# Conditioning vectors of a two-layer diffusion step: dot products spread out, part of them on the matrix engine, deeper weight splitting

## The chip, the cores and the metric

The program runs on one core of a Trainium2 chip. The engines of that core work in parallel, each on its own queue in order: TensorE (PE, with its weight loads shown apart as PEld), VectorE (DVE), ScalarE (ACT), GpSimd (POOL) and SyncE (SP), which here issues almost all transfers. The metric is device time in microseconds (us); lower is better. Three runs of the kernel before took 2530.45, 2533.19 and 2536.13 us, so the median is 2533.19 us.

## The reference

One inference step of a backbone with two layers and a width of D = 2048, over 128 context tokens and 128 latent tokens (256 columns in all). Cut to what matters here:

```
def modulation(cond, w_mod_l, b_mod_l):              # six vectors of 2048 numbers for each
    m = silu(cond) @ w_mod_l + b_mod_l               # layer and each of two conditions
    return split(m, 6)            # shift1, scale1, gate1, shift2, scale2, gate2

def trunk_layer(x, mod, ...):
    q_r, k_r, v_r, g_r, q_a, k_a, v_a = split(modulate(x, shift1, scale1) @ w_in_l)
    y_r = retention_output(...)                      # 8 heads, two directions
    y_a = windowed attention with a sink             # 8 query heads, 2 key/value heads
    x = x + gate1 * (concat(y_r, y_a) @ w_out_l)
    x = x + gate2 * conv_ffn(modulate(x, shift2, scale2), w_up_l, conv_w_l, conv_b_l, w_down_l)
    return x, k_a, v_a, states

modulate(x, shift, scale) = rms_norm(x) * (1 + scale) + shift
```

All of it is float32. The conditioning matrix `w_mod` alone has 2 x 2048 x 12288 numbers, a third of all weights that are read.

## The kernel before, in words

Activations lie transposed: `xT` holds 16 chunks of 128 features by 256 tokens. Each weight matrix is cut into 128 x 128 tiles, 16 tiles to a **unit** of 1 MB that one DMA brings into a slot of `raw` (RAWB = 6 slots, issued in order on SP, each as soon as a slot is given back), and 8 tiles to a **piece**. There are 768 pieces in the program and two pieces in each unit. A float32 product is made of three faster ones: the weight piece is split into a rounded part `hi` (ACT, line 440) and the rest `lo` (DVE, line 441), the operand `hT` (or `ypair`) likewise into columns 0 to 255 and 256 to 511, and `triple` (lines 585 to 587) multiplies hi by hi, hi by lo and lo by hi. So a piece is 24 matmuls of 256 columns. `split_upto` runs LOOK = 2 pieces ahead of the piece being multiplied, and LOOK + 1 = 3 slots hold the split pieces.

The stages follow one another in an order written out in `events`: in each layer the input projection by heads ("kv", "q", "ret"; 88 pieces), the output projection ("out", 32), and three times an up projection ("up", 64, 64 and 48 pieces) and a down projection ("down", 32, 32 and 24). Between "out" and "up", and between the layers, stands a **norm**: the last output chunk is added to `xT` and squared, `norm1` sums the squares on PE (line 478), takes the root on POOL, and `norm2` spreads the factor over the partitions (line 490). Then `emit_h` makes `hT` chunk by chunk, and the first 16 pieces after a norm (two weight groups side by side, `duo_piece`) take the chunks as they come. Smaller work of the heads is done in steps: `step_side` after each piece runs one step of a queue of tasks (`kv_task`, `q_task`, `ret_task`), whose matmuls into `aux` stand in PE's queue between pieces.

The six conditioning vectors of each layer are made in two ways.

- **On PE** (`emit_mod0`, `emit_mod`, lines 359 and 373): a load of 1 MB of `w_mod` is multiplied by the condition, with four matmuls of 512 columns that stand on four strips of 32 columns of the array. Layer 0's first two vectors take 32 such loads before and during the first 48 pieces, gate1 of each layer takes 16 loads more, one at a time.
- **On DVE** (`emit_dot`, line 382): 128 outputs need two dot products (one for each condition) of 2048 products; a load of 1 MB serves both. There are 128 loads and 256 such instructions, for the other eight vectors. `dots` lists them in the order of use, and `dknots` and `quota` say how many must have been issued by which piece. While `hT` is made after a norm none is issued; what the quota asks for by then comes at once behind the last of these pieces.

Of the kernel before, what the change touches and what calls it, by code (L numbers as in the profile page):

```python
# [26 lines left out]
LOOK = 2  # L27
RAWB = 6
# [93 lines left out]
PESEQ = [(0, 2), (1, 2)]  # L122
DVESEQ = [(0, 4), (0, 3), (0, 5), (1, 1), (1, 0), (1, 4), (1, 3), (1, 5)]
# [3 lines left out]
def body(ctx: ExitStack, tc: tile.TileContext, io):  # L127
# [5 lines left out]
    mods = [(l, v, u) for l, v in PESEQ for u in range(MU)]  # L133
    dots = [(l, v, u, k) for l, v in DVESEQ for u in range(KC) for k in range(2)]
# [6 lines left out]
    def mod_event():  # L141

        if issued[0] < len(mods):
            events.append(("mod", mods[issued[0]]))
# [12 lines left out]
    knots = [(ahead, 0), (gstart["out", 0] - 2, MU), (gstart["kv", 1], MU), (gstart["out", 1] - 2, 2 * MU)]  # L157
    nd = 2 * KC
    dknots = [(ahead // 3, 0), (gstart["up", 0] - 4, 2 * nd), (gstart["down", 0] - 6, 3 * nd),
              (gstart["kv", 1] - 6, 11 * nd // 2), (gstart["up", 1] - 4, 7 * nd), (gstart["down", 1] - 6, 8 * nd)]  # L160
# [8 lines left out]

    def startup(b, i):  # L170
        for h in range(MU // 8):
            events.append(("mod0", (0, 1 - i // 2, b, MU // 8 * (i % 2) + h)))
# [14 lines left out]
    for j, p in enumerate(pieces):  # L187
        g = groups[p["it"]["g"]]
        kind, l = g["kind"], g["l"]
        if "gb" in p["it"] and p["first"]:  # L190
            w = 0 if kind == "kv" else 1
            start = j
            events.append(("norm1", None))
            events.append(("norm2", None))
# [4 lines left out]
        if "gb" in p["it"]:  # L199
            for _ in range(2 if (j - start) % 3 == 2 else 1):  # L200
                if chunks:
                    hs.append(chunks.popleft())
            hs = (l, w, hs)
# [29 lines left out]
    for ev, arg in events:  # L233
        if ev in ("mod", "mod0"):
# [28 lines left out]
    dump = one.tile([P, D], BF16, name="dump")  # L263
# [22 lines left out]
    def pump():  # L286
        while nload[0] < len(loads):
# [10 lines left out]
            else:  # L298
                src = io["w_" + key[0]]
                if key[0] == "mod0":  # L300
                    at = key[1]
                else:
                    l, v, u = key[1]
                    at = ((PESEQ if key[0] == "mod" else DVESEQ).index((l, v)), u)
# [20 lines left out]
    def close_mod(ps, l, v, b=None):  # L325

        mod_fin()
        ev = tp.tile([P, 512], F32, tag="t2", name="mev", bufs=3)
# [20 lines left out]
    def emit_mod0(v, b, h):  # L349

        key = ("mod0", (0, v, b, h))
# [11 lines left out]
        if h == MU // 4 - 1:  # L363
            close_mod(md[0], 0, v, b)
# [22 lines left out]
    def end_dots(l, v):  # L387
        dst = modT[l][:, v, :, :]
        bias = C("bmod", l * 96 + v * KC, KC)
        nc.vector.tensor_tensor(dst, dst, bias.unsqueeze(2).to_broadcast([P, KC, 2]), op=ALU.add)  # L390
        if v in (1, 4):
            nc.vector.tensor_scalar_add(dst, dst, 1.0)
# [95 lines left out]
    def norm2():  # L488
        ps = aux()
        nc.tensor.matmul(ps[:, 0:256], ones, diag[0], start=True, stop=True)  # L490
        nc.scalar.copy(rb, ps[:, 0:256])

    hu = {}

    def emit_hu(l, w, kcs, ahead=True):

        m = modT[l]
        for kc in kcs:
# [5 lines left out]
            for s in range(2):  # L504
                a = slice(P * s, P * s + P)
                nc.vector.scalar_tensor_tensor(u[:, a], xT[:, kc, a], m[:, 3 * w + 1, kc, s:s + 1], rb[:, a],
                                               op0=ALU.mult, op1=ALU.mult)

# [21 lines left out]
    def emit_piece(j):  # L530
# [10 lines left out]
        if p["first"]:  # L541
            cur.clear()
            cur["ps"] = [ps_m.tile([P, 512], F32, tag="m", name="acc") for _ in range(2)]
# [3 lines left out]
        for i, (n, kc) in enumerate(p["tiles"]):  # L547
            c = cur["n"]
            out = cur["ps"][n // 2][:, 256 * (n % 2):256 * (n % 2) + 256]
            c[n] += 1  # L550
            src = Y(kc) if g["kind"] in ("out", "down") else hT[:, kc, :]
            triple(out, j, i, src, c[n] == 1 and n % 2 == 0, c[n] == nk)
            if c[n] == nk and n % 2 == 1:
                fin.append(n)
# [3 lines left out]
        for n in fin:  # L558
            evac(gi, g, n, cur["ps"][n // 2])
# [69 lines left out]

    def evac(gi, g, n, ps):  # L630
# [12 lines left out]
        else:  # L643
            nt = g["ns"][n - 1]
            v = 2 if kind == "out" else 5
            t = tp.tile([P, 512], F32, tag="t2", name="gx", bufs=3)
# [389 lines left out]
```

## Time and profile before

| what | value |
|---|---|
| median of three runs | 2533.19 us |
| the profiled execution, its own time | 2530.89 us |
| its span, first to last instruction | 2529.1 us |
| mean granted TensorE clock | 0.979 |
| PE busy | 2381.1 us, 94% |
| DVE busy | 1985.7 us, 79% |
| ACT busy | 1175.9 us, 46% |
| bytes moved | 619.36 MB, mean 245 GB/s |

The profiled execution spends 1.8 us outside its span. A busy engine is not proof of a bound: matmuls overlap, so PE counts as busy as long as one is in flight. What a stage loses is read by comparing it with a like stage that has no wait. "PEclk" is the share of full clock granted to TensorE; its two levels are 2.4 GHz (1.0) and 1.2 GHz (0.5).

### The profile page before, as it was taken

Reading aid. Unit: us, or ns where it says so; the run is one execution under the profiler, and the core shown is the slowest. Engines: PE = TensorE matmul, PEld = TensorE weight load, DVE = VectorE, ACT = ScalarE, POOL = GpSimd, SP = SyncE. Lnnn points to the kernel's source line nnn. Section 1 sums busy time; section 2 is a strip of 40 time slices with the busy share of each in tenths; the row PEclk is TensorE's granted clock in tenths of the full one; section 3 lists DMA queues with packets and bytes.
Section 4 is the critical chain, followed back from the end, with each engine's and each line's share of the span. In section 5 each row is a group of like instructions: output and inputs, shape, how many; then the busy total and the mean of one; then the engine's idle time right before and its main releaser. Section 6 shows DMA issues by size and latency. Waiting matters only on the chain.

```text
span 2529.1 us, 46453 instructions
## 1 busy us (share of the span) xinstructions
PE 2381.1 (94%) x19478; PEld 2289.3 (91%) x19478; DVE 1985.7 (79%) x2696; ACT 1175.9 (46%) x1884; POOL 32.3 (1%) x29
## 2 busy tenths in 40 slices
PE   7998999887999999999988999999699999999997
PEld 4887879887999999999987899998699999999997
DVE  4698888989987999789987777787998456655665
ACT  4534434453444454444553444455344445544554
POOL 0000010000000000000000000000000000000000
PEclk9999999998999999999999999999899999999999
DMA  9997777747776777777756687775576555555551
GB/s 403 359 388 289 289 290 287 267 154 262 259 268 243 258 268 259 259 253 254 255 189 243 239 295 288 275 251 177 212 261 249 184 184 186 184 190 179 196 183 68
DMA packets 91265, 619.36 MB, mean 245 GB/s; under 512 B 10160, under 2 KB 16304, under 8 KB 16944
## 3 DMA queue, kind: packets, MB, share of 16 engines
q1 hardware_dynamic: 83520, 605.21, 66.1%
q10 hardware_dynamic: 7536, 11.19, 1.2%
q8 instruction: 152, 2.49, 0.4%
q14 instruction: 57, 0.47, 0.1%
HBM read 611.64 MB, written 4.72 MB: 244 GB/s over the span
## 4 chain that ended last, share of the span: by engine, by line
PE 74%; DVE 16%; issue 5%; ACT 3%; DMA 2%; POOL 0%; DVEq 0%; SPq 0%; POOLq 0%; ACTq 0%
PE acc L585 24%; PE acc L587 23%; PE acc L586 23%; DVE dump L382 6%; DVE lo L441 5%; DMA raw<-in_w_mod 2%; ACT hi L440 1%; PE md L373 1%; DVE grp L579 1%; PE md L359 1%; ACT pr L760 0%; DVE cv L671 0%; DVE cv L673 0%; PE aux L788 0%; DVE cv L678 0%
## 5 line engine op out<-in xcount | busy, mean ns | idle before, releaser
L587 PE MATMUL acc<-hT,lo 128*128 128x256 f32 x4224 | 1190.2, 282 | 65.3 <-DVE lo L441 65.0
L585 PE MATMUL acc<-hT,hi 128*128 128x256 f32 x4224 | 1203.2, 285 | 6.9 <-ACT hT L519 6.4
L586 PE MATMUL acc<-hT,hi 128*128 128x256 f32 x4224 | 1185.6, 281 | 0.6 <-DVE hT L524 0.6
L441 DVE TENSOR_TENSOR lo<-raw,hi 128x1024 fp32r<-128x1024 f32 x768 | 935.0, 1222 | 301.3 <-ACT hi L440 298.8
L440 ACT CAST hi<-raw 128x1024 fp32r<-128x1024 f32 x768 | 805.2, 1049 | 551.0 <-PE acc L586 439.7
L587 PEld LDWEIGHTS acc<-hT,lo 128*128 128x128 f32 x4224 | 800.1, 189 | 72.8 <-DVE lo L441 72.6
L585 PEld LDWEIGHTS acc<-hT,hi 128*128 128x128 f32 x4224 | 799.8, 189 | 47.1 <-issue 28.1
L586 PEld LDWEIGHTS acc<-hT,hi 128*128 128x128 f32 x4224 | 798.4, 189 | 2.8 <-DVE hT L524 0.9
L382 DVE SCALAR_TENSOR_TENSOR dump<-raw,cbc 128x2048 bf16<-128x2048 f32 x256 | 584.6, 2284 | 0.8
L587 PE MATMUL acc<-ypair,lo 128*128 128x256 f32 x1920 | 544.2, 283 | 4.9 <-DVE lo L441 4.9
L585 PE MATMUL acc<-ypair,hi 128*128 128x256 f32 x1920 | 544.7, 284 | 0.6 <-ACT ypair L684 0.6
L586 PE MATMUL acc<-ypair,hi 128*128 128x256 f32 x1920 | 543.3, 283 | 0.1
L587 PEld LDWEIGHTS acc<-ypair,lo 128*128 128x128 f32 x1920 | 368.4, 192 | 6.4 <-DVE lo L441 6.3
L585 PEld LDWEIGHTS acc<-ypair,hi 128*128 128x128 f32 x1920 | 368.5, 192 | 0.9 <-ACT ypair L684 0.8
L586 PEld LDWEIGHTS acc<-ypair,hi 128*128 128x128 f32 x1920 | 368.4, 192 | 0.4 <-DVE ypair L685 0.3
L670 ACT ACTIVATE cv<-acc,cst 128x256 f32<-128x256 f32 x176 | 98.9, 562 | 240.0 <-DVE cv L673 240.0
L650 ACT ACTIVATE gx<-acc,modT 128x128 f32<-128x128 f32 x256 | 73.2, 369 | 118.0 <-PE acc L587 118.0
L671 DVE SCALAR_TENSOR_TENSOR cv<-acc,cst,cv 128x254 f32<-128x254 f32 x176 | 84.1, 478 | 55.8 <-ACT cv L670 55.8
L652 DVE TENSOR_TENSOR xT<-gx,xT 128x512 f32<-128x512 f32 x64 | 44.2, 691 | 81.6 <-ACT gx L650 81.6
L673 DVE SCALAR_TENSOR_TENSOR cv<-acc,cst,cv 128x254 f32<-128x254 f32 x176 | 84.8, 482 | 6.3
L684 ACT CAST ypair<-cv 128x256 fp32r<-128x256 f32 x88 | 35.6, 405 | 74.0 <-DVE cv L678 74.0
L359 PE MATMUL md<-raw,sc 128*32 128x512 f32 x256 | 36.4, 676 | 16.6 <-ACT sq L455 10.6
(125 smaller groups left out, 896.2 us busy)
## 6 DMA issues: line engine op xcount, KB each, us to landing
raw<-in_w_up SPq DMA_DIRECT2D x176, 1024.0 KB, 4.9
raw<-in_w_dot SPq DMA_DIRECT2D x128, 1024.0 KB, 5.9
raw<-in_w_in SPq DMA_DIRECT2D x88, 1024.0 KB, 6.0
raw<-in_w_down SPq DMA_DIRECT2D x88, 1024.0 KB, 4.9
raw<-in_w_mod SPq DMA_DIRECT2D x64, 1024.0 KB, 7.6
raw<-in_w_out SPq DMA_DIRECT2D x32, 1024.0 KB, 5.2
xT<-in_xT ACTq DMA_DIRECT2D x2, 1024.0 KB, 9.9
s<-in_state ACTq DMA_DIRECT2D x16, 128.0 KB, 4.8
```

The lines of the kernel that those rows point to most:

```text
L359: nc.tensor.matmul(md[0][32 * j:32 * j + 32, :], sc[:, 2 * kc:2 * kc + 32], t[:, 512 * i:512 * i + 512], start=kc < 4, stop=kc >= 12)
L382: nc.vector.scalar_tensor_tensor(dump, raw[key], 1.0, acc[:, k, :], op0=ALU.mult, op1=ALU.mult, accum_out=modT[l][:, v, u, k:k + 1])
L440: nc.scalar.copy(hi, r)
L441: nc.vector.tensor_tensor(lo, r, hi.bitcast(F32), op=ALU.subtract)
L585: nc.tensor.matmul(out, hi, src[:, 0:256], start=first, stop=False, skip_group_check=True)
L586: nc.tensor.matmul(out, hi, src[:, 256:512], start=False, stop=False, skip_group_check=True)
L587: nc.tensor.matmul(out, lo, src[:, 0:256], start=False, stop=last, skip_group_check=True)
L650: nc.scalar.activation(tv[:, i, P * s:P * s + P], pv[:, i, P * s:P * s + P], AF.Copy, scale=modT[l][:, v, nt + i, s:s + 1])
L652: nc.vector.tensor_tensor(xT[:, nt:nt + 2, :], tv, xT[:, nt:nt + 2, :], op=ALU.add)
L670: nc.scalar.activation(t, src, AF.Identity, bias=C("convb", l * 2 * FC + f, 1), scale=w[1])
L671: nc.vector.scalar_tensor_tensor(t[:, :, 1:P], src[:, :, 0:P - 1], w[0], t[:, :, 1:P], op0=ALU.mult, op1=ALU.add)
L673: nc.vector.scalar_tensor_tensor(t[:, :, 0:P - 1], src[:, :, 1:P], w[2], t[:, :, 0:P - 1], op0=ALU.mult, op1=ALU.add)
```

## The change

1. The vectors are dealt out anew. DVE keeps 100 of its 128 loads (200 dot products); a quarter (512 outputs) of four vectors, and the whole of shift2 of layer 0, go to PE, gate1 of layer 1 is made in quarters too. PE has 92 loads of `w_mod` where it had 64.
2. Dot products are planned ahead (`plan`): at most one behind a piece, spread by the room that a stage is given (`DSHARE`) and the piece at which each vector is due; none from 3 pieces before to 12 pieces after the start of a stage that follows a norm.
3. Loads that PE multiplies come in pairs, two behind one piece. Four more stand inside each of three norms, two ahead of `norm1` and two between `norm1` and `norm2`.
4. LOOK is 3 where it was 2 (four slots of split pieces), RAWB is 5 where it was 6.
5. `emit_h2` makes two chunks of `hT` at once: one multiplication of 512 columns on DVE, four scale-and-shift activations and one 512-column copy on ACT, and one 512-column subtraction on DVE.
6. The last two output chunks before a norm have a PSUM bank each and are added to `xT` by DVE alone, straight from PSUM (`evac_one`).
7. In `ffn_pair` the ACT step and the DVE steps of the convolution come one piece apart.
8. The unused product of a dot goes to `hua` instead of a tile of its own; temporaries of 512 columns have four slots instead of three.

```diff
-LOOK = 2
-RAWB = 6
+LOOK = 3
+RAWB = 5
...
-PESEQ = [(0, 2), (1, 2)]
-DVESEQ = [(0, 4), (0, 3), (0, 5), (1, 1), (1, 0), (1, 4), (1, 3), (1, 5)]
+PESEQ = [(0, 2), (0, 3)]
+QMID = [(0, 4, 0), (1, 2, 1), (1, 2, 2), (1, 2, 3)]
+QNORM = {("up", 0): (0, 5, 0), ("kv", 1): (1, 2, 0), ("up", 1): (1, 5, 0)}
+DVESEQ = [(l, v, u) for l, v, n in ((0, 4, 4), (0, 5, 4), (1, 1, 0), (1, 0, 0), (1, 4, 0), (1, 3, 0), (1, 5, 4))
+          for u in range(n, KC)]
+DSHARE = {"kv": 0.38, "q": 0.38, "ret": 0.38, "out": 0.42, "up": 0.36, "down": 0.42}
...
-    dknots = [(ahead // 3, 0), (gstart["up", 0] - 4, 2 * nd), (gstart["down", 0] - 6, 3 * nd),
-              (gstart["kv", 1] - 6, 11 * nd // 2), (gstart["up", 1] - 4, 7 * nd), (gstart["down", 1] - 6, 8 * nd)]
+    due = [gstart[first_use[v], l] - 5 for l, v, u, k in dots]
+        ends = any(gstart[k] - 4 < j <= gstart[k] + 12 for k in QNORM)
+        if j >= ahead and not ends:
+            room[j] = DSHARE[g["kind"]]
...
+        credit = min(credit + room[j] * rate, 2.0)
+        if room[j] and credit >= 1 and nd < len(dots):
+            plan[j], credit, nd = 1, credit - 1, nd + 1
...
+            q = QNORM[kind, l]
+            for h in range(2):
+                events.append(("modq", (*q, h)))
             events.append(("norm1", None))
+            for h in range(2, 4):
+                events.append(("modq", (*q, h)))
             events.append(("norm2", None))
...
-            for _ in range(2 if (j - start) % 3 == 2 else 1):
-                if chunks:
-                    hs.append(chunks.popleft())
+            if (j - start) % 3 != 2:
+                for _ in range(2):
+                    if chunks:
+                        hs.append(chunks.popleft())
...
-        elif not hs:
-            while issued[0] < quota(j, knots):
-                mod_event()
-        if not hs:
-            while issued[1] < quota(j, dknots):
-                dot_event()
+        elif issued[0] + 1 < quota(j, knots):
+            mod_event()
+            mod_event()
+        for _ in range(plan[j]):
+            dot_event()
...
+    def emit_h2(l, w, kc, between):
+        t = tp.tile([P, 2, 256], F32, tag="t2", name="ht", bufs=4)
+        nc.vector.tensor_tensor(t, xT[:, kc:kc + 2, :], rb.unsqueeze(1).to_broadcast([P, 2, 256]), op=ALU.mult)
+        between()
+        for i in range(2):
+            for s in range(2):
+                nc.scalar.activation(t[:, i, a], t[:, i, a], AF.Identity, bias=m[:, 3 * w, kc + i, s:s + 1],
+                                     scale=m[:, 3 * w + 1, kc + i, s:s + 1])
+        hi = hT[:, kc:kc + 2, 0:256]
+        nc.scalar.copy(hi, t)
+        nc.vector.tensor_tensor(hT[:, kc:kc + 2, 256:512], t, hi.bitcast(F32), op=ALU.subtract)
...
+    def evac_one(g, nt, ps):
+        for s in range(2):
+            nc.vector.scalar_tensor_tensor(xT[:, nt, a], ps[:, a], modT[l][:, v, nt, s:s + 1], xT[:, nt, a],
+                                           op0=ALU.mult, op1=ALU.add)
+        fresh.append(once(square_out if g["kind"] == "down" and l == DEPTH - 1 else square, nt))
```

What stands in the engines' queues, first on DVE behind the 16 pieces that follow layer 0's first norm (`cv` is the convolution of the up projection, `lo` a split piece, `dump` or `hua` the unused product of a dot). Before:

```order
L671 SCALAR_TENSOR_TENSOR cv<-acc,cst,cv 128x2x127
L673 SCALAR_TENSOR_TENSOR cv<-acc,cst,cv 128x2x127
L382 SCALAR_TENSOR_TENSOR dump,modT<-raw,cbc 128x2048 x9
L441 TENSOR_TENSOR lo<-raw,hi 128x1024
L685 TENSOR_TENSOR ypair<-cv,ypair 128x256
L678 TENSOR_TENSOR cv<-cv 128x256
L441 TENSOR_TENSOR lo<-raw,hi 128x1024
L685 TENSOR_TENSOR ypair<-cv,ypair 128x256
L382 SCALAR_TENSOR_TENSOR dump,modT<-raw,cbc 128x2048
L441 TENSOR_TENSOR lo<-raw,hi 128x1024 x2
```

The same place on DVE now:

```order
L746 SCALAR_TENSOR_TENSOR cv<-acc,cst,cv 128x2x127
L410 SCALAR_TENSOR_TENSOR hua,modT<-raw,cbc 128x2048
L470 TENSOR_TENSOR lo<-raw,hi 128x1024
L758 TENSOR_TENSOR ypair<-cv,ypair 128x256
L751 TENSOR_TENSOR cv<-cv 128x256
...
L470 TENSOR_TENSOR lo<-raw,hi 128x1024
L758 TENSOR_TENSOR ypair<-cv,ypair 128x256
L751 TENSOR_TENSOR cv<-cv 128x256
L410 SCALAR_TENSOR_TENSOR hua,modT<-raw,cbc 128x2048
L470 TENSOR_TENSOR lo<-raw,hi 128x1024
```

Nine dot products in a row ahead of one split piece have become single ones with a split piece between them.

On PE around layer 0's first norm (`acc` is a piece, `md` a load of `w_mod`, 8 matmuls for two loads). Before:

```order
L587 MATMUL acc<-ypair,lo 128x256
L478 MATMUL aux<-mean,ssq 128x1
L478 MATMUL aux<-mean,sq 128x1
L478 MATMUL aux<-mean,ssq 128x1
L478 MATMUL aux<-mean,sq 128x1
L490 MATMUL aux<-dg,ones 128x256
L585 MATMUL acc<-hT,hi 128x256
```

The same place on PE now:

```order
L639 MATMUL acc<-ypair,lo 128x256
L387 MATMUL md<-raw,sc 32x512 x8
L507 MATMUL aux<-mean,ssq 128x1
L507 MATMUL aux<-mean,sq 128x1
L507 MATMUL aux<-mean,ssq 128x1
L507 MATMUL aux<-mean,sq 128x1
L387 MATMUL md<-raw,sc 32x512 x8
L519 MATMUL aux<-dg,ones 128x256
L637 MATMUL acc<-hT,hi 128x256
```

Two loads stand ahead of the sums of squares, and two ahead of the matmul that spreads the factor.

On SP, the transfers of layer 0's output projection (one row is 1 MB for each "x1"). Before:

```order
L297 DMA raw<-in_w_out 128x2048 x2
L307 DMA raw<-in_w_dot 128x2048
L297 DMA raw<-in_w_out 128x2048
L307 DMA raw<-in_w_dot 128x2048
L297 DMA raw<-in_w_out 128x2048 x2
L307 DMA raw<-in_w_dot 128x2048
```

The same stage on SP now:

```order
L326 DMA raw<-in_w_out 128x2048
L335 DMA raw<-in_w_mod 128x2048 x2
L326 DMA raw<-in_w_out 128x2048
L335 DMA raw<-in_w_dot 128x2048
L326 DMA raw<-in_w_out 128x2048
L335 DMA raw<-in_w_mod 128x2048 x2
L326 DMA raw<-in_w_out 128x2048
```

Between the units of the projection now stand two loads for PE at a time, beside those for the dots.

## Rows read from the trace of the kernel before

**Rows 1.** Busy time by stage: window, us, engines, PEclk, DMA share, GB/s.

```profile
33.60:204.10 170.50, 166.80 (x1368) 146.53 (x1369) 139.24 (x214) 78.29 (x109) 0.00 (x0) 0.98 0.97 385
204.10:393.70 189.60, 170.40 (x1297) 145.67 (x1296) 160.84 (x269) 73.87 (x144) 12.47 (x7) 0.98 0.78 287
393.70:503.40 109.70, 99.72 (x800) 97.23 (x798) 99.69 (x121) 51.03 (x92) 3.29 (x2) 0.97 0.75 270
503.40:720.80 217.40, 188.79 (x1537) 185.43 (x1538) 198.33 (x279) 98.20 (x154) 0.00 (x0) 0.94 0.64 227
720.80:813.00 92.20, 92.20 (x771) 92.20 (x770) 75.03 (x74) 42.28 (x64) 0.00 (x0) 1.00 0.71 259
813.00:994.70 181.70, 181.31 (x1538) 180.95 (x1537) 167.56 (x207) 91.03 (x128) 0.00 (x0) 1.00 0.71 256
...
1223.20:1305.50 82.30, 73.27 (x588) 71.44 (x586) 71.37 (x108) 43.71 (x83) 0.69 (x1) 0.96 0.67 236
1305.50:1400.10 94.60, 84.31 (x651) 78.39 (x651) 77.07 (x136) 43.05 (x86) 0.00 (x0) 0.94 0.60 215
1400.10:1622.60 222.50, 220.69 (x1802) 205.39 (x1800) 167.29 (x244) 96.10 (x153) 12.53 (x7) 1.00 0.76 276
...
1726.30:1943.00 216.70, 188.18 (x1536) 185.02 (x1537) 197.78 (x279) 98.22 (x154) 0.00 (x0) 0.94 0.64 227
```

**Rows 2.** Waits of PE, whole span: who waits for whom, us, times, longest.

```profile
PE acc L587 <- DVE lo L441: 69.9, 37, 21.6
...
PE md L359 <- DMA raw<-in_w_mod: 6.0, 6, 2.0
...
PE aux L775 <- DVE pr L768: 6.9, 2, 5.8
...
PE md L373 <- DMA raw<-in_w_mod: 2.7, 1, 2.7
```

**Rows 3.** DVE in order of time behind layer 0's first norm: start, duration, instruction.

```profile
559.93 2.28 DVE L382 SCALAR_TENSOR_TENSOR dump<-raw,cbc 128x2048 bf16<-128x2048 f32 x1
...
578.59 2.29 DVE L382 SCALAR_TENSOR_TENSOR dump<-raw,cbc 128x2048 bf16<-128x2048 f32 x1
580.80 0.08 DVE L382 DVE_READ_ACCUMULATOR dump<-raw,cbc 128x1 f32 x1
580.80 1.22 DVE L441 TENSOR_TENSOR lo<-raw,hi 128x1024 fp32r<-128x1024 f32 x1
```

**Rows 4.** Costliest groups of the page: count, busy us, mean ns, idle before.

```profile
L440 ACT CAST hi<-raw 128x1024 fp32r<-128x1024 f32 x768 | 805.2, 1049 | 551.0 <-PE acc L586 439.7
L382 DVE SCALAR_TENSOR_TENSOR dump<-raw,cbc 128x2048 bf16<-128x2048 f32 x256 | 584.6, 2284 | 0.8
```

**Rows 5.** The chain that ended last: start, us, what.

```profile
54.57 1.85 PE md L359 x16
...
1511.50 1.00 PE md L373 x8
```

**Rows 6.** In order of time around the second norm, between the layers.

```profile
1296.62 1.14 ACT L650 ACTIVATE gx<-acc,modT 128x128 f32<-128x128 f32 x4 [1.89 <-PE acc L587]
1297.79 0.69 DVE L652 TENSOR_TENSOR xT<-gx,xT 128x512 f32<-128x512 f32 x1 [1.13 <-ACT gx L650]
...
1299.45 0.48 PE L478 MATMUL aux<-mean,ssq 128*128 128x1 f32 x2 [2.87 <-DVE ssq L459]
...
1302.73 1.22 PE L490 MATMUL aux<-dg,ones 128*128 128x256 f32 x2 [1.52 <-ACT dg L485]
...
1304.39 0.61 DVE L506 SCALAR_TENSOR_TENSOR hu<-xT,modT,rb 128x128 f32<-128x128 f32 x2 [1.83 <-ACT rb L491]
1304.78 0.69 ACT L519 ACTIVATE hT<-hu,modT 128x128 fp32r<-128x128 f32 x2 [0.42 <-DVE hu L506]
...
1305.52 0.58 PE L585 MATMUL acc<-hT,hi 128*128 128x256 f32 x1 [1.57 <-ACT hT L519]
```

**Rows 7.** PE in order of time at the start, where loads arrive back to back.

```profile
14.53 1.94 PE L359 MATMUL md<-raw,sc 128*32 128x512 f32 x8 [1.98 <-DMA raw<-in_w_mod]
17.01 1.94 PE L359 MATMUL md<-raw,sc 128*32 128x512 f32 x8 [0.54 <-DMA raw<-in_w_mod]
```

More of the change, by code (lines that the diff above doesn't have):

```diff
@@ L132, in body @@
     events = []
-    mods = [(l, v, u) for l, v in PESEQ for u in range(MU)]
-    dots = [(l, v, u, k) for l, v in DVESEQ for u in range(KC) for k in range(2)]
+    mods = [("mod", (l, v, u)) for l, v in PESEQ for u in range(MU)]
+    mods += [("modq", (*q, h)) for q in QMID for h in range(MU // 4)]
+    dots = [(*d, k) for d in DVESEQ for k in range(2)]
     issued = [0, 0]
@@ L168, in quota @@
         return knots[-1][1]
+    first_use = {0: "kv", 1: "kv", 2: "out", 3: "up", 4: "up", 5: "down"}
+    due = [gstart[first_use[v], l] - 5 for l, v, u, k in dots]
+    room = [0.0] * len(pieces)
+    for j, p in enumerate(pieces):
+        g = groups[p["it"]["g"]]
+        ends = any(gstart[k] - 4 < j <= gstart[k] + 12 for k in QNORM)
+        if j >= ahead and not ends:
+            room[j] = DSHARE[g["kind"]]
+    plan, credit, nd = [0] * len(pieces), 0.0, 0
+    for j in range(len(pieces)):
+        while nd < len(dots) and due[nd] <= j:
+            plan[j], nd = plan[j] + 1, nd + 1
+        rate = max([sum(x <= d for x in due[nd:]) / max(sum(room[j:d]), 0.1) for d in sorted(set(due[nd:]))], default=0)
+        credit = min(credit + room[j] * rate, 2.0)
+        if room[j] and credit >= 1 and nd < len(dots):
+            plan[j], credit, nd = 1, credit - 1, nd + 1
     def startup(b, i):
         for h in range(MU // 8):
-            events.append(("mod0", (0, 1 - i // 2, b, MU // 8 * (i % 2) + h)))
+            events.append(("modq", (0, 1 - i // 2, b, MU // 8 * (i % 2) + h)))
     for i in range(4):
@@ L542, in emit_piece @@
             cur.clear()
-            cur["ps"] = [ps_m.tile([P, 512], F32, tag="m", name="acc") for _ in range(2)]
+            cur["ps"] = [None] * 4
             cur["n"] = [0] * 4
@@ L548, in emit_piece @@
             c = cur["n"]
-            out = cur["ps"][n // 2][:, 256 * (n % 2):256 * (n % 2) + 256]
+            single = g["ns"][n] >= KC - 2 and last_add(g)
+            b = n if single else n // 2 * 2
+            if cur["ps"][b] is None:
+                cur["ps"][b] = ps_m.tile([P, 512], F32, tag="m", name="acc")
+            out = cur["ps"][b][:, 256 * (n - b):256 * (n - b) + 256]
             c[n] += 1
             src = Y(kc) if g["kind"] in ("out", "down") else hT[:, kc, :]
-            triple(out, j, i, src, c[n] == 1 and n % 2 == 0, c[n] == nk)
-            if c[n] == nk and n % 2 == 1:
-                fin.append(n)
+            triple(out, j, i, src, c[n] == 1 and n == b, c[n] == nk)
+            if c[n] == nk and (single or n % 2 == 1):
+                fin.append((n, cur["ps"][b], single))
             if i == PIECE // 2 - 1 and len(side) > 1:
@@ L557, in emit_piece @@
         del hi_t[j], lo_t[j]
-        for n in fin:
-            evac(gi, g, n, cur["ps"][n // 2])
+        for n, ps, single in fin:
+            if single:
+                evac_one(g, g["ns"][n], ps)
+            else:
+                evac(gi, g, n, ps)
         run_later()
@@ L628, in run_later, with last_add @@
         fresh.clear()
+    def last_add(g):
+        return g["kind"] == "out" or g["kind"] == "down" and g["last"]
+    def evac_one(g, nt, ps):
+        l, v = g["l"], 2 if g["kind"] == "out" else 5
+        for s in range(2):
+            a = slice(P * s, P * s + P)
+            nc.vector.scalar_tensor_tensor(xT[:, nt, a], ps[:, a], modT[l][:, v, nt, s:s + 1], xT[:, nt, a],
+                                           op0=ALU.mult, op1=ALU.add)
+        fresh.append(once(square_out if g["kind"] == "down" and l == DEPTH - 1 else square, nt))
+        if nt == KC - 1:
+            ytile.clear()
     def evac(gi, g, n, ps):
@@ L653, in evac @@
             for i in range(2):
-                if kind == "out" or g["last"]:
+                if last_add(g):
                     fresh.append(once(square_out if kind == "down" and l == DEPTH - 1 else square, nt + i))
@@ L663, in ffn_pair @@
         o = []
-        cv = tp.tile([P, 2, 2, P], F32, tag="t2", name="cv", bufs=3)
+        cv = tp.tile([P, 2, 2, P], F32, tag="t2", name="cv", bufs=4)
+        for k in range(2):
+            f = c + k * FC
+            src = pv[:, k, :].rearrange("p (s t) -> p s t", s=2)
+            t = cv[:, k, :, :]
+            w = C("convw", (l * 3 + 1) * 2 * FC + f, 1)
+            nc.scalar.activation(t, src, AF.Identity, bias=C("convb", l * 2 * FC + f, 1), scale=w)
+        yield True
         for k in range(2):
```

68 lines of the change are left out of this document (36 added, 32 removed).

## The prediction

> **What bounds the kernel now.** I read the busy times by stage first, then who PE waits for, then the order of time at the two kinds of place where it waits. The stages show a floor [rows 1]. The first down projection of layer 0 (720.8 to 813.0, 32 pieces) takes 92.20 us with PE busy throughout: 2.88 us for a piece. The second up projection (813.0 to 994.7, 64 pieces) takes 181.70 us. Its twin right behind the norm, the same 64 pieces, takes 217.40 us in layer 0 and 216.70 in layer 1. Those two are 35.7 and 35.0 us too long, and both have PE idle for some 28 us (window less PE busy) and a granted clock of 0.94. The heads are too long as well: 204.1 to 393.7 has 40 pieces, or 115.2 us of floor, and takes 189.6.
>
> The waits name the releaser: of all that PE waits for, 69.9 us in 37 waits end with a split weight (`lo`) from DVE, the longest 21.6 us [rows 2]. The order of time shows which DVE work stands ahead: nine dot products in a row from 559.93 to 580.80, then the `lo` that PE wants [rows 3]. At 2.284 us each [rows 4] nine are 20.6 us, and PE has three split pieces, 8.6 us, in hand at best. So the bound is PE, with holes cut by bursts of DVE; DVE's total of 79% is not the trouble.
>
> **The change, part by part.** The sum is made against the profiled execution: 2530.89 us, of which 2529.1 are span, 2.3 under the median of 2533.19.
>
> *Bursts behind the norms.* The new order on DVE has no two dots without a split piece between, and PE has four pieces, 11.5 us, in hand. A dot and a `lo` take 2.28 + 1.22 us and come about every 7 us in these stages. The clean twin already carries dots at that density (26 in 64 pieces; the new plan has 21 and 19) without a wait, so I give both up stages 181.7 + 0.8 us, the 0.8 for a first piece at low clock: -34.9 and -34.2. The start of layer 1 (1305.5 to 1400.1) has the same sickness: 10.3 us idle, and 0.94 of the clock, which is 12% of 94.6 us at half speed, so 5.5 us lost. Four single loads, 4.0 us, move out of it. Leaving 1.5 us of waits: -18.3.
>
> *Loads on PE.* A pair takes 1.85 us on the chain, a single load 1.00 [rows 5]; with the restart of the pieces I take 1.89 a pair. PE has 92 loads for 64. Of the 28 new ones 12 stand inside norms; layer 0 gets 20 more in its heads and output projection, layer 1 loses 4. Layer 0 from 204.1 to 503.4 had 299.3 us. Its floor is 72 x 2.88 = 207.4. The heads' own small matmuls I take from layer 1 (1305.5 to 1622.6): 317.1, less 88 x 2.88, less 16 loads of 1.0, less 15.8 and 1.8 of idle and lost clock, leaves 30. Eighteen pairs are 34.0. The norm is below, 9.9. For waits that stay I put 12: 5 in the heads, where a softmax result from DVE cost 5.8 us at one place [rows 2] and fewer dots (17 for 26) stand ahead, and 7 for transfers. Sum 293.3: -6.0. The six pairs in layer 1's heads for twelve singles, and one wait less: -1.5.
>
> *Transfers.* In layer 0's output projection the 28 pieces up to the norm need 14 units, 20 loads for PE and 6.5 for dots: 40.5 MB-sized loads, 42.5 MB in 28 x 2.88 + 10 x 1.89 + 3.7 = 103 us, or 412 GB/s. The fastest long stretch moved 385 GB/s at a DMA share of 0.97 [rows 1], which makes it 110 us: 7 us of waits. From the other side, loads at the start come 2.48 us apart [rows 7], which would be 100 us and no wait. I take the long stretch, since it is the one with pieces in it.
> The Trainium skill speaks against this stage more sharply: "DMA: Bandwidth & Descriptors", Specifications, puts HBM at about 358 GB/s for a core. By that the stage would take 118.6 us, 8 more than I take; the trace disagrees, with 385 GB/s held over 170 us [rows 1].
>
> *Slots.* RAWB falls by one, and a dot load now keeps its slot for the two or three pieces between its two products. With four slots left for units, each worth 5.76 us, a unit is asked for some 17 us ahead; I cost this at nothing, and at up to 1 us a place where a load for PE follows one held slot.
>
> *Norms.* Between the layers the last matmul ends near 1296.6 and the first of the next stage starts at 1305.52: 8.9 us, and the stage then starts at half clock [rows 6]. The new path ahead of the sums, two 128x128 DVE operations (0.61 for such a pair) and a square, is shorter than the 2.83 us from 1296.62 to 1299.45, but two loads (1.85) stand there. The sums take 1.8 at low clock, 1.1 at full. Then the root and its spreading, 1.5 idle, are covered by two loads of 1.85. From 1302.73 to 1305.52 nothing changes: 2.8. So 1.85 + 1.1 + 1.85 + 2.8 = 7.6, and I take 7.9 with the four loads inside for nothing; without cover they would cost 3.7. In layer 0's norm transfers run late: 9.9. In layer 1's a half-used dot holds a slot, so the fourth load is asked for only when PE has used the first: 9.9. The stage 1223.2 to 1305.5 was 82.30 for 24 pieces (69.1): with 7.9, and without late `lo`s, -5.3; layer 1's norm +1.0.
>
> *Operand in 512-column steps.* For two chunks DVE had eight operations of 128 columns, 2.4 us by the 0.61 pair; now two of 512 at 0.69. ACT had 4 x 0.35 and has that plus a 512-column copy (0.4 to 0.7) and the split's cast, 1.05 [rows 4, 6]: 3.1 us. The loop activations, copy, subtraction, next multiplication is about 3.7 us in two of three pieces and 1.2 in the third: 8.6 against PE's 8.64. It just fits with four pieces in hand: nothing. Uncovered it is 0.8 us a step, 21 steps, 17 us.
>
> *Rest.* The first 48 pieces lose their 19 dots and some waits for loads (6.0 us in all for these loads): -2.5. The dense stages in between get slightly more dots and a longer `ffn_pair`: +1.6. The tail is shorter by an evacuation and a square: -1.4.
>
> Sum: -34.9 - 34.2 - 18.3 - 6.0 - 1.5 - 5.3 + 1.0 - 2.5 + 1.6 - 1.4 = -101.5, so 2429.4. Between this and the median's level I say **2430 us**.
>
> **Rivals.** *Loads become the wait.* PE's queue is in order, so a pair whose data is late stops pieces that are ready. For it: 412 GB/s asked in one stage, one slot fewer. Against it: 270 to 290 GB/s elsewhere [rows 1]. Waits for loads so far were 1.0 us on average and 2.7 at most [rows 2]. At 24 pairs and 3 norms, 1.35 us each is 36 us: 2466.
>
> *DVE's relief doesn't reach PE.* The operand steps do not fit (17 us), and the heads' waits are chains through DVE and ACT that fewer dots don't shorten (10 us): 2457. For it: a softmax wait of 5.8 us; against it: layer 1's heads (1400.1 to 1622.6) idle only 1.8 us at 0.4 dots a piece.
>
> *Slower than before.* The same queueing behind late loads, at a price that eats everything: 27 places would have to stop PE for 3.8 us each. That is above the longest wait seen (2.7), but the clock falls after a long stop (0.94 in the stages with them [rows 1]), which could add to it: 2540 at 4.1 us a place.
>
> **How the numbers follow.** The forecast 62%, its own range 2414 to 2446 from the unknown terms (transfers 0 to 15, norms 3 to 6, heads 0 to 10); loads 20%; relief lost 14%; slower 3%; no effect 1%. The range 2410 to 2468 leaves out the far end of the two middle cases. A measurement of this kernel tells 0.2% (5 us) from no change: faster 0.95, same 0.015, slower 0.035.
>
> **What would show it.** Right: the up stages behind the norms at 182 to 184 us with a clock of 1.00; no wait for `lo` above 2 us; layer 1's start near 76 us; norms of 8 to 10 us with `md` matmuls inside. Wrong: `md` waiting for transfers more than 20 us in all; `hT` among PE's waits in the pieces behind a norm; layer 0's output projection above 125 us with its norm.

## The result and the profile after

The changed kernel takes 2463.01 us (median of four runs, 2459.25 to 2466.46) where the kernel before takes 2533.35 us (four runs): a ratio of 0.9722 with a 95% interval of 0.9704 to 0.9741. So it is faster, by 70 us, and 33 us slower than the 2430 forecast. The profiled execution of the changed kernel took 2464.25 us, its span is 2462.4: 66.7 us less than before, where the sum of the steps said 101.5. The miss to be explained is 34.8 us.

Busy time by stage, after, in the same columns as [rows 1]. Each row is the same work as the row of [rows 1] that stands in its place; the windows run from a stage's first piece to the next stage's first piece.

```profile
33.20:204.20 171.00, 168.00 (x1368) 147.16 (x1369) 106.21 (x183) 78.97 (x110) 0.00 (x0) 0.97 0.88 334
204.20:386.90 182.70, 167.70 (x1298) 146.62 (x1296) 136.65 (x242) 74.03 (x144) 6.75 (x7) 0.98 0.68 251
386.90:523.60 136.70, 124.89 (x1001) 101.91 (x998) 87.37 (x116) 51.52 (x91) 1.38 (x2) 0.98 0.97 377
523.60:707.40 183.80, 183.80 (x1541) 183.70 (x1542) 165.56 (x218) 106.93 (x161) 0.00 (x0) 0.99 0.69 246
...
1208.30:1289.10 80.80, 75.87 (x621) 71.33 (x619) 72.76 (x113) 43.00 (x80) 0.69 (x1) 1.00 0.71 260
1289.10:1370.40 81.30, 78.39 (x623) 76.06 (x623) 55.80 (x81) 49.96 (x93) 0.00 (x0) 0.98 0.55 197
1370.40:1589.40 219.00, 218.95 (x1809) 206.78 (x1808) 173.23 (x254) 97.36 (x155) 12.53 (x7) 1.00 0.77 283
...
1695.40:1878.70 183.30, 183.29 (x1540) 183.19 (x1541) 163.47 (x215) 106.48 (x161) 0.00 (x0) 0.99 0.68 243
```

Both up stages behind a norm now have PE busy for the whole window, 183.8 and 183.3 us, where they had 28 us of idle time and 0.94 of the clock. Layer 0's heads and output projection, the second and third row, are the place where the forecast went wrong: 182.7 + 136.7 = 319.4 us, longer than the 299.3 before. Against the steps of the prediction:

| stretch | before | forecast | after | miss |
|---|---|---|---|---|
| first 48 pieces | 170.5 | 168.0 | 171.0 | +3.0 |
| layer 0: heads, output projection, norm | 299.3 | 293.3 | 319.4 | +26.1 |
| layer 0: up behind the norm | 217.4 | 182.5 | 183.8 | +1.3 |
| last down of layer 0 with the norm | 82.3 | 77.0 | 80.8 | +3.8 |
| layer 1: start | 94.6 | 76.3 | 81.3 | +5.0 |
| layer 1: other heads | 222.5 | 221.0 | 219.0 | -2.0 |
| layer 1: output projection, norm | 103.7 | 104.7 | 106.0 | +1.3 |
| layer 1: up behind the norm | 216.7 | 182.5 | 183.3 | +0.8 |
| dense stages, start, tail | 1122.1 | 1122.3 | 1117.8 | -4.5 |

Waits of PE after, whole span, as in [rows 2]:

```profile
PE md L387 <- DMA raw<-in_w_modq: 14.5, 12, 2.8
...
PE md L401 <- DMA raw<-in_w_mod: 7.0, 6, 1.6
PE acc L637 <- ACT hT L564: 6.5, 4, 1.7
PE aux L945 <- DVE ro L940: 5.8, 5, 2.2
PE aux L848 <- DVE pr L841: 3.8, 2, 2.6
...
PE acc L639 <- DVE lo L470: 2.7, 3, 1.3
```

The 69.9 us for `lo` have become 2.7, in three waits of at most 1.3 us. Waits for loads that PE multiplies have grown from 8.7 us to 21.5. Most of what is left besides these is one wait of 10.0 us at the start of the program (10.6 before), the chains of the heads (`ro`, `pr`) and the start of a stage (`hT`). DVE in order of time where nine dots stood in a row [rows 3]:

```profile
564.38 1.23 DVE L470 TENSOR_TENSOR lo<-raw,hi 128x1024 fp32r<-128x1024 f32 x1 [1.60 <-ACT hi L469]
565.52 2.28 DVE L410 SCALAR_TENSOR_TENSOR hua<-raw,cbc 128x2048 bf16<-128x2048 f32 x1
...
567.74 1.22 DVE L470 TENSOR_TENSOR lo<-raw,hi 128x1024 fp32r<-128x1024 f32 x1
```

DVE now waits for ACT ahead of the split (1.60 us): it has time to spare, and one dot of 2.28 us is followed by a split piece at once.

A cast still takes 1051 ns on average and a dot 2284, as in [rows 4]; there are 200 dots for 256. The norm between the layers on PE [rows 6]:

```profile
1281.13 1.92 PE L387 MATMUL md<-raw,sc 128*32 128x512 f32 x16
...
1283.45 0.38 PE L507 MATMUL aux<-mean,ssq 128*128 128x1 f32 x2 [0.40 <-DVE ssq L488]
...
1284.43 1.06 PE L387 MATMUL md<-raw,sc 128*32 128x512 f32 x8
...
1286.78 0.70 PE L519 MATMUL aux<-dg,ones 128*128 128x256 f32 x2
...
1289.06 0.39 PE L637 MATMUL acc<-hT,hi 128*128 128x256 f32 x1 [1.57 <-ACT hT L564]
```

A pair is one run of 1.92 us where two loads were foreseen at 1.85 [rows 5]; the first piece starts at 1289.06, 8.14 us after the start of the last matmul of the stage before (7.86 after its end, which is what the 7.9 of the forecast counts). Its first matmul runs at full clock (0.39 us where [rows 6] has 0.58); then the clock falls all the same, to a mean of 0.59 from 1289.1 to 1293.3 us.

### The profile page after: what moved, and what is told of

Its sections match the earlier page's. It is cut to its first block, busy times and chain, and to the rows that moved or that the text cites. A ratio compares the mean times of both kernels' runs of the same rounds, so it can differ in the third digit from the quotient of the medians.

```text
span 2462.4 us, 46787 instructions
## 1 busy us (share of the span) xinstructions
PE 2389.6 (97%) x19730; PEld 2289.1 (93%) x19730; DVE 1842.0 (75%) x2484; ACT 1201.9 (49%) x1896; POOL 24.7 (1%) x29
## 4 chain that ended last, share of the span: by engine, by line
PE 86%; DVE 6%; DMA 5%; ACT 2%; issue 1%; SPq 0%; POOL 0%; ACTq 0%; DVEq 0%; POOLq 0%
PE acc L637 27%; PE acc L639 27%; PE acc L638 27%; DMA raw<-in_w_modq 2%; DVE lo L470 2%; PE md L387 2%; DMA raw<-in_w_mod 2%; DVE hua L410 2%; ACT hi L469 1%; PE md L401 1%; ACT pr L833 1%; DMA raw<-in_w_in 0%; PE aux L861 0%; DVE st L825 0%; PE aux L442 0%
## 5 line engine op out<-in xcount | busy, mean ns | idle before, releaser
L469 ACT CAST hi<-raw 128x1024 fp32r<-128x1024 f32 x768 | 806.0, 1051 | 698.7 <-PE acc L638 585.8
L637 PEld LDWEIGHTS acc<-hT,hi 128*128 128x128 f32 x4224 | 797.8, 189 | 33.8 <-issue 18.3
L410 DVE SCALAR_TENSOR_TENSOR hua<-raw,cbc 128x2048 bf16<-128x2048 f32 x200 | 456.7, 2284 | 6.6 <-DMA raw<-in_w_dot 6.6
L387 PE MATMUL md<-raw,sc 128*32 128x512 f32 x480 | 65.8, 654 | 24.5 <-DMA raw<-in_w_modq 14.5
L737 ACT ACTIVATE cv<-acc,cst 128x256 f32<-128x256 f32 x176 | 89.4, 558 | 0.0
L387 PEld LDWEIGHTS md<-raw,sc 128*32 128x32 f32 x480 | 11.9, 113 | 53.1 <-DMA raw<-in_w_modq 28.4
```

What stands on the lines that cost most here:

```text
L387: nc.tensor.matmul(md[0][32 * j:32 * j + 32, :], sc[:, 2 * kc:2 * kc + 32], t[:, 512 * i:512 * i + 512], start=kc < 4, stop=kc >= 12)
L410: nc.vector.scalar_tensor_tensor(hua.rearrange("p c t -> p (c t)").bitcast(BF16), raw[key], 1.0, acc[:, k, :], op0=ALU.mult, op1=ALU.mult, ...
L469: nc.scalar.copy(hi, r)
L637: nc.tensor.matmul(out, hi, src[:, 0:256], start=first, stop=False, skip_group_check=True)
L737: nc.scalar.activation(t, src, AF.Identity, bias=C("convb", l * 2 * FC + f, 1), scale=w)
```

## The experiments

The theory after this result: the spreading of the dots gives what was forecast, and the miss lies in slots (RAWB 5) and in layer 0's heads and norms. Each edit is made on the changed kernel.

**Dots in bursts again.** A quota asks for them behind the norm's pieces, as before; all else stays.

```diff
-        for _ in range(plan[j]):
-            dot_event()
+        if "gb" not in p["it"]:
+            while issued[1] < quota(j, dknots):
+                dot_event()
```

> The changed kernel with one part undone: the 200 dot products are issued by a quota again, so 6, 7 and 6 of them come at once behind the pieces that follow three norms; everything else is as changed. If the spreading is what paid (my theory), the bursts of 14 to 16 us against 11.5 us of split pieces in hand give waits of 5 to 10 us and a fall of the clock at three places: 2490 to 2510 us, with waits for lo of over 5 us. If the deeper splitting or the fewer dots paid (rival), bursts of this size are covered: within 8 us of 2463.

Measured: 2500.55 us, ratio 0.9875 (0.9858 to 0.9891). Its first up stage behind a norm (the second took 195.1 us), and the two longest sums of PE's waits that the order of the dots bears on:

```profile
519.40:715.00 195.60, 186.02 (x1540) 185.50 (x1541) 174.08 (x223) 106.11 (x161) 0.00 (x0) 0.96 0.66 236
```

```profile
PE acc L643 <- DVE lo L474: 20.5, 5, 8.8
PE aux L852 <- DVE pr L845: 17.8, 3, 15.2
```

As expected of the spreading (2490 to 2510 us). So some 37 of the 70 us come from the order of the dots alone: 11.8 us in each of the two up stages, and most of the rest in the start of layer 1, where a burst falls on a softmax result (one wait of 15.2 us). The bursts here are six or seven dots, against nine before. The other 33 us come with the 56 dots fewer and the rest of the change, which no run takes apart.

**Depth against slots.** Two split pieces ahead and six slots, as before the change, with everything else changed:

```diff
-LOOK = 3
-RAWB = 5
+LOOK = 2
+RAWB = 6
```

> The changed kernel with split pieces three deep and six load slots, as in the kernel before; dots stay spread. If the spreading alone takes the waits for lo away (my theory), 2463 to 2470 us. If the depth is needed to carry a dot and a split piece (rival), waits for lo come back in the up stages: 2485 us or more. If the missing sixth slot is what holds the output projection of layer 0 back, that stage with its norm falls from 136.7 us to 130 or less.

Measured: 2449.41 us, ratio 0.9674 (0.9660 to 0.9689), 14 us better than the change itself and below what spreading alone was expected to give (2463 to 2470); the clause on slots, the output projection under 130 us, held. Its profiled execution took 2444.49 us, 4.9 under its median, so the stages below show more than the medians do. Its stages from the first 48 pieces to the first up stage:

```profile
34.20:200.00 165.80, 165.37 (x1368) 146.16 (x1369) 104.97 (x182) 78.20 (x110) 0.00 (x0) 0.98 0.89 345
200.00:382.60 182.60, 166.95 (x1296) 145.29 (x1295) 136.72 (x242) 73.96 (x144) 8.65 (x7) 0.99 0.68 255
382.60:507.20 124.60, 122.34 (x1000) 102.12 (x998) 87.18 (x116) 51.66 (x91) 1.38 (x2) 1.00 0.98 397
507.20:691.70 184.50, 182.52 (x1540) 181.71 (x1541) 165.61 (x218) 106.91 (x161) 0.00 (x0) 1.00 0.70 253
```

The first 48 pieces gain 5.2 us and layer 0's output projection 12.1, while the heads and the up stage stay where they were. How far one profile can be trusted shows in two kernels further down, which have the change's own instructions up to there: the first 48 pieces took 171.0, 172.2 and 169.1 us in the three, the output projection with its norm 136.7, 136.8 and 134.1, the norm alone 10.58, 12.19 and 9.39. PE in order of time at layer 0's norm, first of the change, then of this kernel:

```profile
513.19 1.92 PE L387 MATMUL md<-raw,sc 128*32 128x512 f32 x16
...
516.46 1.07 PE L387 MATMUL md<-raw,sc 128*32 128x512 f32 x8 [0.36 <-DMA raw<-in_w_modq]
518.90 1.94 PE L387 MATMUL md<-raw,sc 128*32 128x512 f32 x8 [1.38 <-DMA raw<-in_w_modq]
520.77 1.22 PE L519 MATMUL aux<-dg,ones 128*128 128x256 f32 x2
```

```profile
500.25 1.92 PE L387 MATMUL md<-raw,sc 128*32 128x512 f32 x16
...
503.09 1.92 PE L387 MATMUL md<-raw,sc 128*32 128x512 f32 x16
504.94 0.70 PE L519 MATMUL aux<-dg,ones 128*128 128x256 f32 x2
```

In the change the third and fourth load come late, one by one, PE stands for 1.38 us, and the fourth load and the spreading matmul then run at half clock (1.94 for 1.06, 1.22 for 0.70). With six slots and two pieces ahead they are one run of 16. From the last piece to the next all three norms of this kernel take 7.18 us; in the change they take 10.58, 8.14 and 11.62. Five slots with LOOK = 2 separate the two numbers:

> The changed kernel with split pieces three deep, but still five load slots: it splits the two halves of the run with three deep and six slots (2449.4 us, 14 below the changed kernel). If the slot given up is what that run won back (theory A), this one stays at 2463 to 2475 us, with layer 0's output projection and norm at 130 us or more and norms of 10 to 12 us that wait for loads. If the deeper splitting itself costs (theory B, each unit is taken from its slot no later but asked for earlier), this one falls to 2450 to 2455 us.

Measured: 2457.81 us, ratio 0.9708 (0.9692 to 0.9724), between the two theories. Its layer 0's output projection, the third and fourth load of that norm, and the waits for the pairs:

```profile
381.90:514.70 132.80, 123.25 (x1001) 101.75 (x999) 87.29 (x116) 51.72 (x91) 1.38 (x2) 1.00 0.96 374
```

```profile
510.49 1.97 PE L387 MATMUL md<-raw,sc 128*32 128x512 f32 x16
```

```profile
PE md L401 <- DMA raw<-in_w_mod: 7.6, 7, 1.6
```

The norms take 7.22, 7.37 and 7.99 us. So five slots alone do not make the loads in the norms late: with two pieces ahead they are in time, and what was lost there came with the depth of three. The pairs in layer 0's output projection wait as in the change (7.6 us for 7.0), and the sixth slot takes this to 0.6 and the stage from 132.8 to 124.6. So of the 14 us about 8 belong to the sixth slot and about 5 to the smaller depth; the interval overlaps that of the change, so the second share is less sure than the first. LOOK = 3 with six slots was not run, so the slot's worth at that depth is open. In the kernel's order of loads, LOOK = 3 puts one more unit ahead of the four loads of each norm; that they are late for this reason is likely, but no run isolates it. The other end, LOOK = 1 and RAWB = 7:

> The change with LOOK = 1 (two slots of split pieces, two pieces or 5.76 us in hand) and RAWB = 7. Theory: the gain from RAWB 5 to 6 came from loads that were asked for too late, and with six slots only 0.6 us of such waits is left in layer 0's output projection, so a seventh slot brings little there (124 us or a little less with its norm; first 48 pieces 162 to 166 us); what is given up is depth: a dot of 2.28 us and a split of 1.22 us, with the convolution's steps beside them, must then fit under 5.76 us, and waits for lo come back in the up stages behind the norms (188 to 195 us each instead of 181 to 185) and at the operand's steps. 2455 to 2485 us in all. Rival: slots are worth more than depth at every step, the up stages stay at 181 to 185 us, waits for lo stay near 10 us, and it is 2435 to 2448 us.

Measured: 2633.95 us, ratio 1.0403 (1.0385 to 1.0420): waits for `lo` came back as expected, but at 185 us over LOOK 2, where 6 to 36 were expected, and layer 0's output projection, expected at 124, took 129.1. Its first up stage, the dense down stage behind it, and PE's longest sum of waits:

```profile
528.40:727.10 198.70, 187.10 (x1540) 183.12 (x1541) 166.53 (x217) 107.02 (x161) 0.00 (x0) 0.99 0.66 234
727.10:828.20 101.10, 95.30 (x771) 92.85 (x770) 78.34 (x75) 42.41 (x64) 0.00 (x0) 1.00 0.67 242
```

```profile
PE acc L639 <- DVE lo L470: 131.2, 155, 2.7
```

Even a stage without a norm, 92.1 us in the change, takes 101.1. Of the 155 waits 94, 103 of the 131 us, end with a split piece that stood right behind a dot; the 570 us after the last dot have 21 short ones, 7.2 us in all. So with one piece ahead about every second dot stops PE a little; with two a single dot mostly fits (12 waits, 9.5 us), and with three nothing more is won. Depth is a step here, not a slope. PE's busy time grew too, by 71 us over LOOK 2 (2378.0 to 2449.4), which no run explains.

**No dots in layer 0's heads.** The 17 dots before the output projection are left out, with the loads that only they use (`modT` is filled with zeros).

```diff
         for _ in range(plan[j]):
-            dot_event()
+            if j < gstart["out", 0]:
+                issued[1] += 1
+            else:
+                dot_event()
```

> The changed kernel, with the 17 dot products behind the pieces of layer 0's heads left out, and their loads (part of scale2 is then not computed). The heads of layer 0 took 182.7 us where 166 were forecast. If dots stand in the chains that PE waits for there (theory A), the stage falls by 10 us or more, and the waits for ro, pr and ra by half or more. If the steps of the heads' tasks simply stand half a piece apart, too close for their chains through ACT, DVE and POOL (theory B), the stage falls by less than 5 us and these waits stay above 8 us in all.

Measured, one execution: 2452.76 us; the heads take 174.4 us where the change has 182.7, a fall between those of the two theories, and the waits stay above 8 us, as theory B has it. PE's waits in these 40 pieces, first of the change (204.2 to 386.9), then without dots (202.6 to 377.0):

```profile
PE aux L945 <- DVE ro L940: 5.8, 5, 2.2
PE aux L861 <- ACT pt L850: 2.7, 3, 1.8
PE aux L848 <- DVE pr L841: 2.6, 1, 2.6
PE aux L916 <- ACT ra L904: 1.8, 2, 1.3
PE aux L926 <- DVE rk L913: 1.7, 3, 0.6
```

```profile
PE aux L948 <- DVE ro L943: 3.9, 5, 0.9
PE aux L864 <- ACT pt L853: 2.9, 3, 1.8
PE aux L929 <- DVE rk L916: 1.1, 3, 0.6
PE aux L851 <- DVE pr L844: 0.5, 1, 0.5
```

A dot in the heads, with its share of a load, costs 8.3 / 17 = 0.5 us of PE's time. Of 14.9 us of waits (a sixth row has 0.3), 8.4 stay with no dot at all: by the names in the rows they are the chains themselves, through ACT and DVE.

**No loads in the norms.** The 12 loads that stand inside the three norms are left out.

```diff
-            for h in range(2):
-                events.append(("modq", (*q, h)))
             events.append(("norm1", None))
-            for h in range(2, 4):
-                events.append(("modq", (*q, h)))
```

> The changed kernel without the twelve loads inside the three norms (a quarter of three vectors is then not computed). If they cost nothing there (my forecast), the norm between the layers stays within 1 us of the 8.1 us from last matmul to first, and the clock of the pieces behind it falls to 1.2 GHz for longer. If they are on the path (rival), each norm is 1.9 to 3.7 us shorter. Layer 1's norm, where the third load waits 2.8 us for its data, falls from 11.4 to 8 or 9 us in both cases.

Measured, one execution: 2451.97 us; norms of 6.05, 8.35 and 6.58 us. The norm between the layers stays within 1 us, as forecast; there PE waits 2.26 us for a sum of squares that DVE makes. The clock behind it is lower, 0.73 in the first 9 us for 0.81. Layer 1's norm fell further than the 8 or 9 us expected. With four loads in time a norm is 7.18: the loads cost at most about 1 us in it. It is their lateness that costs more, 3.4 us in layer 0 and 4.4 in layer 1 over those 7.18.

**An even number of dots ahead of each norm,** so that no half-used load holds a slot there.

```diff
+        last = any(j == gstart[k] - 4 for k in QNORM)
-        if room[j] and credit >= 1 and nd < len(dots):
+        if room[j] and (nd % 2 if last else credit >= 1) and nd < len(dots):
```

> The changed kernel, with the plan of dots closed on an even count three pieces ahead of each norm, so that no half-used dot load holds a slot through layer 1's norm. If that slot is why the norm's third load is late there (my forecast), the norm falls from 11.6 to about 9 us and its wait for data from 2.8 to 0.5 us or less. If the slot plays no part (rival), 11.6 us stays.

Measured, one execution: 2462.94 us. Layer 1's norm falls from 11.62 to 8.01 us, so the held slot was real; with LOOK = 2 and the same five slots it cost less than 1 us (7.99 us with the odd count, beside 7.22 and 7.37). The count was even before the other two norms already, and layer 0's 12.19 us for 10.58 are the same instructions run again.

**The operand one chunk at a time,** by the old routine, in place of `emit_h2`.

```diff
-                    emit_h2(hs[0], hs[1], hs[2][0], lambda: split_upto(j + LOOK + 1))
+                    emit_h(*hs, between=lambda: split_upto(j + LOOK + 1))
```

> The changed kernel with the operand after a norm made by the old routine, chunk by chunk, two chunks in a call. My forecast gave the 512-column steps nothing, so 2463 us within 4. If they carry part of the gain (rival), the up stages behind the norms rise from 183.5 to 187 us or more and the total by 8 us. If they cost (ACT as the chain), the total falls.

Measured: 2462.76 us, ratio 0.9727 (0.9712 to 0.9741). No difference that can be told: the 512-column steps neither gain nor lose.

**A version from these results:** LOOK 2 and RAWB 6, 12 loads of layer 0's shift2 back on DVE, dots from piece 17 on, the even number, and a tile of its own for the dots' unused product in place of the fourth temporary.

```diff
-LOOK = 3
-RAWB = 5
+LOOK = 2
+RAWB = 6
...
-        if j >= ahead and not ends:
+        if j >= ahead // 3 and not ends:
```

> A version made from these findings: three deep with six slots, twelve of PE's loads (three quarters of shift2 of layer 0) back on DVE, and dots allowed from piece 17 on, into a tile of their own, where DVE is busy 106 of 171 us. PE saves 12 x 0.95 us, the output projection of layer 0 asks for fewer loads; the first 48 pieces ask for 7.5 more, near the fastest rate seen. If loads on PE and the rate in one stage are the price (theory), 2434 to 2442 us. If dots in layer 0's heads cost as much as they save there (half a us each, by the run without them; rival), 2445 to 2452 us.

Measured: 2443.24 us, ratio 0.9650 (0.9636 to 0.9665), between the ranges of theory and rival, and the fastest kernel of this study, though its interval overlaps that of LOOK 2 and RAWB 6 alone. Layer 0's output projection and first up stage:

```profile
388.30:503.20 114.90, 111.40 (x905) 100.52 (x902) 91.33 (x120) 51.34 (x91) 2.26 (x2) 0.99 0.87 333
503.20:691.70 188.50, 185.23 (x1540) 184.63 (x1541) 172.36 (x222) 107.27 (x161) 0.00 (x0) 0.98 0.70 252
```

Against LOOK 2 and RAWB 6 the output projection loses another 9.7 us, and the stages that now carry the dots give it back, 4.0 in this up stage, 3.2 in the first 48 pieces and 3.5 in the heads: moved work was mostly paid for elsewhere. The two profiled executions are 1.2 us apart.

## Why the forecast was right in kind and 33 us too low

The measured 2463 us lies 17 us above the forecast's own range (2414 to 2446) and inside the whole one (2410 to 2468) because that was drawn to take in most of two rivals. The spreading did what was forecast. Part of the nearness is luck: late loads were priced at about their size, for a wrong cause.

**Bursts: right.** Both up stages came within 1.3 us of the forecast, no wait for `lo` exceeds 1.3 us, and with bursts again the two stages lose a third of what they had gained. Whether the rest comes from shorter bursts, the depth or the fewer dots is not taken apart; with the dots spread, depth adds nothing. The clock is 0.99 where 1.00 was expected.

**Slots: a cost put at nothing.** "I cost this at nothing, and at up to 1 us a place where a load for PE follows one held slot" was wrong. Put back, with the depth it was paid for, the slot is worth 14 us by the medians (2463.0 to 2449.4), most of it where loads for PE stand: of the 19.7 us between the two profiles 12.1 lie in layer 0's output projection with its norm, 4.4 in layer 1's, and perhaps 5.2 in the first 48 pieces; other stages give some back. The argument looked at units alone (17 us ahead) and not at the loads for PE, which share the slots and come in groups. Yet this is not what the 33 us are made of. The sum held 11 us for late loads under other names, 7 as transfers and 2 in each of two norms (9.9 for 7.9), and with six slots the kernel still takes 19 us more than the 2430 forecast. And the depth that the slot bought has no use once dots come one at a time: with two pieces ahead PE waits 9.5 us for `lo` in place of 2.7, and the up stages are no slower (184.5 and 181.6).

**Transfers: right size, wrong cause.** The 7 us of waits came out as 9.9 in that stage (7.0 for its pairs, 2.9 for the quarter loads), but not because 412 GB/s can't be had. With six slots nearly the same bytes (rate times time: 49.5 MB for 51.5) moved at 397 GB/s in 124.6 us, with 0.6 us of waits for loads in the stage, so what this stage needs can be had. That the limit was how far ahead a load could be asked for follows for the sixth slot, which alone took the waits away. No run moved 412 GB/s, and the DMA share is 0.96 to 0.98 with five slots and with six: there is little to spare in either.

**Layer 0's heads: the step that failed most.** The whole stretch is 26.1 us over its 293.3. PE's waits in it are 25.9 us, where 12 were put for the heads and the transfers and 3.3 are part of the norm as forecast: about 10 us over, nearly all in the heads (14.9 for 5). The other 15 us or so stand in no wait. They come from the floor: "The heads' own small matmuls I take from layer 1 ... leaves 30". The stretch before could have been read directly: 299.3 less 27.5 us of waits is 271.8 with 16 loads, and 20 loads more at 0.95 make 291, against the 278 that the borrowed floor gives without the norm's waits. In layer 1 the tasks' steps stand a whole piece apart; in layer 0 several tasks are queued, `step_side` also runs in the middle of a piece, and each step's chain through ACT and DVE has only half a piece, 1.44 us, to finish. That part of the 13 us is lost in restarts is likely but only argued; the granted clock of 0.98 in both windows allows at most 6 us. And the twin was not one: layer 1's window holds the tasks of seven retention heads (14 matmuls L945), this stretch those of eight (16). By the busy times of their matmuls in layer 1 (26.0 us for seven) the eighth is worth up to 3.7 us, an estimate.

**Layer 1's start** was to gain 18.3 us and gained 13.3. Idle time fell by 7.4 us (8.8 forecast), and PE's busy time by 5.9, of which 4.0 are the four loads that left: 1.9 are what the clock can have given, for the 5.5 forecast. Half clock before stood in two places:

```profile
1305.50:1309.80 4.30, 4.28 (x19) 4.18 (x20) 4.03 (x13) 2.23 (x5) 0.00 (x0) 0.50 0.02 4
1374.70:1381.50 6.80, 4.45 (x21) 4.45 (x22) 6.36 (x10) 2.58 (x10) 0.00 (x0) 0.50 0.84 307
```

The second went away, but 2.4 us of it were idle and already counted as a wait; of the first, 3.4 us are still there behind the norm.

**Norms: right where the data was there.** From the end of the last matmul, as the forecast counts, they take 0.28 us less than the numbers above: 7.86 us against 7.9 between the layers; 10.30 and 11.34 against 9.9 in the other two, and 6.90 in all three with six slots and two pieces ahead. The held slot in layer 1 was named for the right reason, as the even number shows.

**Small terms.** The pair (1.92 us for 1.89) and the 512-column steps (nothing) were right. The first 48 pieces lost 19 dots and gained nothing; with two pieces ahead they take 165.8 us with six slots and 167.4 with five, so the depth of three is the likelier cause. The 2.7 us of waits for `lo` that are left all lie in layer 0's last down stage and are most of its 3.8.

**The rivals.** Of the three, "loads become the wait" came nearest, in part: waits for loads passed the 20 us named as a sign, and the output projection with its norm passed 125 us (136.7). Its price of 36 us was too high, since waits for loads grew by 12.8 us; before they were 1.2 us on average (8.7 in seven), not 1.0. The end at 2463, near its 2466, is a sum of this and of the heads. "DVE's relief doesn't reach PE" (2457) was half right: 8.4 us of waits in layer 0's heads stay with no dot there, near the 10 it named, while the operand steps cost nothing.

## What to carry to other kernels

Work on an in-order engine that only has to be done by some date is spread until a single piece of it fits into what the next engine has in hand; in this kernel depth beyond that bought nothing, and one piece less cost at about every second dot. A slot given up for depth is priced by the loads that come in groups, not by the steady stream. The floor of a stage is read from that stage itself, span less waits, before one is borrowed from its twin, and the twin's tasks are counted first.

## What the runs showed of the hardware

**A root of two numbers on POOL takes 0.69 us, or 2.60 beside a dot.** The change, in order of time:

```profile
336.30 2.28 DVE L410 SCALAR_TENSOR_TENSOR hua<-raw,cbc 128x2048 bf16<-128x2048 f32 x1
336.53 2.60 POOL L937 TENSOR_TENSOR grs<-grs,mhalf 128x2 f32<-128x2 f32 x1 [14.44 <-DVE grs L936]
...
338.51 1.22 DVE L470 TENSOR_TENSOR lo<-raw,hi 128x1024 fp32r<-128x1024 f32 x1
...
339.65 0.60 DVE L940 TENSOR_SCALAR ro<-ro,ag,grs 128x128 f32<-128x128 f32 x2
...
340.13 0.49 PE L945 MATMUL aux<-cst,ro 128*128 128x128 f32 x2 [2.15 <-DVE ro L940]
```

The root ends half a microsecond after the dot that began 0.23 us ahead of it. In the traces before and after all 14 such roots of the retention heads that last 2.60 us or more begin inside a dot, and none of the 18 short ones does. The Trainium skill, "SBUF — State Buffer", SBUF: two separate sides, says that VectorE and GpSimd share a pair of ports that one of them holds for a whole instruction, an operation of VectorE with two inputs in SBUF among them; this trace agrees. In layer 0's heads five of eight roots were slow before and one of eight is now. The slow root itself cost PE nothing: DVE's queue held the dot and a split piece, to 339.73 us, ahead of the step that reads the root, and that step follows with no idle time in all 14. PE's 2.15 us here are the wait for the dot and the split.

**One core moved 397 GB/s for 124.6 us,** with a DMA share of 0.98, above the 385 of [rows 1].

**How much half clock costs depends on what PE does in it.** Before, layer 0's first up stage had 23.9 us at half clock from 562.3 to 586.2, with 4.1 us of matmuls in them, the rest a wait; in layer 1's start PE was busy for 8.7 of the 11.1 us at half clock.
